# A gated MLP's gate and up projections with tokens as the stationary operand, turned back through 32x32 transposes and DRAM

## The chip, the cores and the metric

The kernel runs on one core of one Trainium2 chip. The metric is the device time of one execution in microseconds (us). The engines are TensorE (PE: matmuls; PEld: its weight loads), VectorE (DVE), ScalarE (ACT), GpSimd (POOL) and SyncE (SP). DMAs are issued by SP and by ACT, and one set of 16 DMA engines carries them all.

## The reference

A trunk of two layers works on 256 tokens of width 2048, in float32: a mixer (layer 0: short convolution and a state-space scan; layer 1: windowed attention), cross-attention into 256 memory tokens, and a gated MLP of width 5632. The change is in the MLP:

```python
def causal_dwconv(u, w):
    L = u.shape[1]
    up = jnp.pad(u, ((0, 0), (CONV_WIDTH - 1, 0), (0, 0)))
    y = up[:, 0:L] * w[0]
    for k in range(1, CONV_WIDTH):
        y = y + up[:, k:k + L] * w[k]
    return y

def conv_gated_mlp(h, w_gate, w_up, conv_w, conv_b, w_down):
    g = causal_dwconv(h @ w_gate, conv_w) + conv_b
    return (jax.nn.silu(g) * (h @ w_up)) @ w_down
```

`h` here is the residual after an RMS norm; the MLP's result is added to the residual. The convolution runs along the tokens, three wide, with weights and a bias of its own for each of the 5632 channels.

## The kernel before, in words

Activations lie with channels on the 128 partitions and the 256 tokens along a partition. A float32 product is made of three float32r products: operands are split into hi and lo, and hi x hi, hi x lo and lo x hi are summed. An activation tile `op` holds hi in its first 256 columns and lo in its last 256 (`split_gain`, L67 and L68; `split`, L74 and L75). Weights come from HBM in pieces of 1 MB or less: `wload` (L78) issues the load on SP into one of three `raw` buffers, ACT makes `hi` (L90) and DVE makes `lo` (L91), four buffers of 1024 columns each. So a load can start when the DVE subtract has read a raw buffer, and a cast when the matmuls have read a hi buffer.

`gemm` (L119) takes one output tile of 128 channels after another. For each it runs, over K contraction tiles, a matmul with the weight's hi stationary and all 512 columns of `op` moving (`mm_hi`, L105), and then one with the weight's lo stationary and the 256 hi columns moving (`mm_lo`, L110). The two halves of the PSUM bank are added by ACT and DVE (`add_halves`, L160 and L161). PSUM has four such banks (`pp`).

The norm's factor per token is not known when the projections begin. `stat_col` (L178) sums the squares on PE (L186) and takes the inverse root; `stat_bc` (L207) spreads it over partitions as `rbc`. In the MLP (`mlp`, L909) the first two tiles are held one contraction tile short (`late`, `pre`), with `stat_col` behind them. GpSimd multiplies gate by `rbc` (L918); ACT and DVE do the convolution (L920 to L922) and ACT the silu (L923); GpSimd multiplies by `rbc` again (L924) and then up by gate (L930); the product is split (L74, L75) into `ops`.

The 44 tiles of the width go in four slabs of 11. The down projection of a slab (16 output tiles, 11 contraction tiles each) adds to the residual `h` (`resid_part`, L961 and L962); the last slab of a layer also begins the next norm (`resid_evac`: L288, L289, `stat_add` with L174 on ACT and L172 on GpSimd, and `split_gain`). One pair of the next slab is computed ahead of each down projection.

The memory's V projection (`mem_kv`, L311 to L329) is of another form: tokens are stationary and 512 weight columns move (L319, L320, L324), into two banks.

A scheduler orders the instructions of every engine before the run; an engine takes its queue in that order, and an instruction that waits holds those behind it. This is so for DMA issues too.

## Time and profile before

| | |
|---|---|
| median of three runs | 2825.39 us (2824.67 to 2825.44) |
| the profiled execution | 2825.51 us |
| its span, first to last instruction | 2823.7 us |
| granted TensorE clock | 0.997 |
| DMA moved | 536.74 MB, mean 190 GB/s |
| 1 MB weight load, issue to landing | 4.8 us |

A profile row names the line, the engine, the operation, the tiles written and read, the shapes, the count, the busy time and the mean length of one in ns; behind the second bar stands the engine's idle time ahead of these instructions and what ended most of it. A timeline row begins with the start and the length in us. Lengths of matmuls are modelled and overlap; the distance of starts is what one costs.

### The profile page before, as it was taken

The page shows a single profiled execution, that of the slowest core. Times are in us where ns is not written, and L with a number is a line of the kernel's source. Part 1 is how long each engine was busy: PE and PEld are TensorE (multiplying, and loading weights), DVE is VectorE, ACT ScalarE, POOL GpSimd, SP SyncE. Part 2 cuts the span into 40 slices and gives each one's busy share as a digit, 9 for nine tenths or more (in the row PEclk, how much of TensorE's full clock was granted, in tenths as well). Part 3 has the DMA queues.
Part 4 walks back from the last instruction along what each step waited for, and adds up shares of the span by engine and source line. Part 5 has one row for each costly group of instructions (what it writes and reads, how often), then busy time and mean ns, then how long its engine had stood idle before and what let it go on. Part 6 is the DMA issues. An engine that isn't in the chain of part 4 may idle for free.

```text
span 2823.7 us, 43952 instructions
## 1 busy us (share of the span) xinstructions
PE 2797.2 (99%) x17159; PEld 2487.4 (88%) x17159; DVE 1956.9 (69%) x3171; ACT 1566.1 (55%) x2520; POOL 358.2 (13%) x397
## 2 busy tenths in 40 slices
PE   9999999999999999999999999999999999999998
PEld 8988979998988888888888888889888888888887
DVE  8878778767766666666666778776666666666666
ACT  7676766655555545545445566555555455454454
POOL 1000000001001211202112310000122012021122
PEclk9999999999999999999999999999999999999999
DMA  8564655555545555455555554454455554654544
GB/s 304 203 220 166 214 213 191 206 181 203 190 174 185 193 169 212 176 199 192 170 204 179 193 183 152 163 209 179 166 193 185 174 208 166 208 193 167 206 171 143
DMA packets 89794, 536.74 MB, mean 190 GB/s; under 512 B 10640, under 2 KB 17136, under 8 KB 38640
## 3 DMA queue, kind: packets, MB, share of 16 engines
q1 hardware_dynamic: 86656, 524.66, 52.7%
q10 hardware_dynamic: 2928, 9.26, 0.8%
q8 instruction: 134, 2.20, 0.3%
q14 instruction: 76, 0.62, 0.1%
HBM read 523.35 MB, written 10.53 MB: 189 GB/s over the span
## 4 chain that ended last, share of the span: by engine, by line
PE 93%; DVE 3%; ACT 2%; DMA 1%; issue 0%; SPq 0%; POOL 0%; DVEq 0%; ACTq 0%; POOLq 0%
PE ps L105 49%; PE ps L110 28%; PE ps L102 3%; PE ps L103 2%; PE ps L319 2%; PE ps L320 2%; PE ps L324 2%; DVE lo L91 1%; PE m L881 1%; ACT stmp L489 1%; PE m L787 1%; DVE stmp L493 1%; DMA kv<-kst 1%; ACT hi L90 0%; DVE S L494 0%
## 5 line engine op out<-in xcount | busy, mean ns | idle before, releaser
L91 DVE TENSOR_TENSOR lo<-raw,hi 128x1024 fp32r<-128x1024 f32 (+2 forms) x1033 | 1202.0, 1185 | 408.4 <-ACT hi L90 151.6
L105 PE MATMUL ps<-op,hi 128*128 128x512 f32 x6101 | 1471.5, 392 | 1.9 <-DVE op L75 1.1
L90 ACT CAST hi<-raw 128x1024 fp32r<-128x1024 f32 (+2 forms) x1033 | 1002.7, 983 | 818.1 <-PE ps L105 694.1
L105 PEld LDWEIGHTS ps<-op,hi 128*128 128x128 f32 x6101 | 1117.9, 188 | 220.9 <-issue 3.2
L110 PEld LDWEIGHTS ps<-op,lo 128*128 128x128 f32 x7008 | 900.4, 191 | 33.5 <-DVE lo L91 1.6
L110 PE MATMUL ps<-op,lo 128*128 128x256 f32 x7008 | 920.5, 283 | 1.4 <-DVE lo L91 1.4
L172 POOL TENSOR_TENSOR acc<-acc,t 128x256 f32<-128x256 f32 x98 | 89.4, 912 | 1194.7 <-ACT t L174 1190.7
L102 PE MATMUL ps<-op,hi 128*128 128x256 f32 x907 | 223.6, 286 | 6.7 <-ACT hi L90 6.6
L103 PE MATMUL ps<-op,hi 128*128 128x256 f32 x907 | 221.4, 284 | 0.0
L102 PEld LDWEIGHTS ps<-op,hi 128*128 128x128 f32 x907 | 174.8, 193 | 10.1 <-ACT hi L90 8.5
L103 PEld LDWEIGHTS ps<-op,hi 128*128 128x128 f32 x907 | 174.9, 193 | 0.1
L160 ACT COPY t<-ps 128x256 f32<-128x256 f32 x234 | 86.4, 372 | 151.6 <-PE ps L110 148.8
L918 POOL TENSOR_TENSOR t<-t,rbc 128x256 f32<-128x256 f32 x88 | 68.6, 780 | 749.2 <-DVE t L161 721.4
L921 DVE SCALAR_TENSOR_TENSOR t<-t,ff_conv 128x255 f32<-128x255 f32 x88 | 42.9, 488 | 141.9 <-ACT t L920 141.9
L924 POOL TENSOR_TENSOR t<-t,rbc 128x256 f32<-128x256 f32 x88 | 109.2, 1240 | 216.5 <-ACT t L923 216.5
L68 DVE SCALAR_TENSOR_TENSOR op<-h,gains,op 128x256 fp32r<-128x256 f32 x96 | 73.0, 768 | 88.4 <-ACT op L67 88.2
L489 ACT ACTIVATE stmp<-S,s_pw 128x256 f32<-128x256 f32 (+3 forms) x256 | 118.4, 530 | 28.3 <-DVE S L496 24.9
L75 DVE TENSOR_TENSOR op<-t,op 128x256 fp32r<-128x256 f32 x104 | 43.9, 424 | 116.6 <-ACT op L74 116.5
L319 PE MATMUL ps<-hi,op 128*128 128x512 f32 x256 | 101.0, 394 | 0.3 <-ACT hi L90 0.3
L320 PE MATMUL ps<-hi,op 128*128 128x512 f32 x256 | 99.9, 390 | 0.0
L161 DVE TENSOR_TENSOR t<-ps,t 128x256 f32<-128x256 f32 x226 | 93.9, 416 | 0.0
L930 POOL TENSOR_TENSOR t<-t 128x256 f32<-128x256 f32 x88 | 66.8, 759 | 135.1 <-DVE t L161 134.8
(213 smaller groups left out, 1705.7 us busy)
## 6 DMA issues: line engine op xcount, KB each, us to landing
raw<-in_ff_gate SPq DMA_DIRECT2D x88, 1024.0 KB, 4.8
raw<-in_ff_up SPq DMA_DIRECT2D x88, 1024.0 KB, 4.8
raw<-in_ff_down SPq DMA_DIRECT2D x128, 704.0 KB, 4.1
raw<-in_xa_k SPq DMA_DIRECT2D x32, 1024.0 KB, 4.9
raw<-in_xa_v SPq DMA_DIRECT2D x32, 1024.0 KB, 4.9
raw<-in_xa_q SPq DMA_DIRECT2D x32, 1024.0 KB, 4.8
raw<-in_xa_o SPq DMA_DIRECT2D x32, 1024.0 KB, 4.8
raw<-in_ev_w_in SPq DMA_DIRECT2D x28, 1024.0 KB, 4.9
```

The lines of the kernel that those rows point to most:

```text
L90: nc.scalar.copy(hi, s)
L91: nc.vector.tensor_tensor(lo, s, hi.bitcast(F32), op=ALU.subtract)
L102: nc.tensor.matmul(ps[:, :T], lhsT=hi, rhs=o[:, :T], start=k == 0, stop=False)
L103: nc.tensor.matmul(ps[:, :T], lhsT=hi, rhs=o[:, T:], start=False, stop=False)
L105: nc.tensor.matmul(ps, lhsT=hi, rhs=o, start=k == 0, stop=False)
L110: self.nc.tensor.matmul(ps[:, :T], lhsT=w[k][1], rhs=ops[k][:, :T], start=False, stop=k == K - 1)
L161: self.nc.vector.tensor_tensor(out, ps[:, :T], t, op=ALU.add)
L172: nc.gpsimd.tensor_tensor(self.acc, self.acc, self.sq, op=ALU.add)
L319: nc.tensor.matmul(ps[b], lhsT=o[:, b * P:(b + 1) * P], rhs=w[j][0], start=k == 0, stop=False)
L320: nc.tensor.matmul(ps[b], lhsT=o[:, T + b * P:T + (b + 1) * P], rhs=w[j][0], start=False, stop=False)
L489: nc.scalar.activation(tmp[:, x, :, p - p0, :], at(0, both, p), AF.Copy, scale=pw[:, x, k, 8 * b + p:8 * b + p + 1])
L924: nc.gpsimd.tensor_tensor(y, y, self.rbc, op=ALU.mult)
```

## The change

Tiles 0 to 39 of gate and up (of 44) take the form of the V projection. `tok_gemm` loads 512 weight columns for four contraction tiles at a time (the same 1 MB as before) and runs, for the even and the odd tokens (b), two matmuls of 512 columns with the weight's hi moving (x hi and x lo stationary) and one with its lo moving. Even and odd tokens are picked by every second column of `op` (`tokens`). Both products go to the same bank, so `add_halves` falls away for them, and the norm's factor is applied per partition by ACT as it evacuates (`tok_turn`). The result has tokens on partitions: DVE transposes it in 32x32 blocks, four DMAs on ACT's queue write it to DRAM (`zd`, runs of 256 bytes), and one DMA on SP's queue reads it back (`zf`, runs of 1 KB) with channels on partitions. The convolution, silu, product and split follow on `zf`, without the products with `rbc`. Tiles 40 to 43 stay in the old form, so `rbc` is still made, with its tokens in order again.

The slabs become 12, 12, 12 and 8 tiles: chunks (of four tiles) 0 to 3, down of 0 to 11; chunks 4 to 6, down; chunks 7 to 9, down; four old pairs, down of the last eight. `stat_col` comes behind the first quarter of the first chunk.

```diff
--- before.py
+++ after.py
@@ -26,7 +26,7 @@
 KT = 16
 DFF = 5632
 NFF = 44
-SLAB = 11
+NTOK = 40
 EPS = 1e-5
 MAGIC = 12582912.0
 XSCALE = 512 ** -0.5
@@ -49,6 +49,7 @@
         self.pp = pool("pp", 4, space=PSUM)
         self.pm = pool("pm", 4, space=PSUM)
         self.dp = pool("dram", 1, space=DRAM)
+        self.dz = pool("dramz", 4, space=DRAM)
     def t1(self, shape=(P, T), dt=F32):
@@ -155,6 +156,47 @@
             n, w, ps = start(i, K)
             finish(n, ps)
+    @staticmethod
+    def tokens(x, b):
+        return x.rearrange("p (m b) -> p b m", b=2)[:, b]
+    def tok_gemm(self, src, xs, after=None):
+        nc = self.nc
+        ps = [self.pp.tile([P, 512], F32, name="ps", tag="ps") for _ in range(2)]
+        for q in range(4):
+            w = self.wload(src(q), 4, 512)
+            for j in range(4):
+                k = 4 * q + j
+                for b in range(2):
+                    for i in range(2):
+                        nc.tensor.matmul(ps[b], lhsT=self.tokens(xs[k][:, i * T:(i + 1) * T], b), rhs=w[j][0], start=k == 0 and i == 0, stop=False)
+            for j in range(4):
+                k = 4 * q + j
+                for b in range(2):
+                    nc.tensor.matmul(ps[b], lhsT=self.tokens(xs[k][:, :T], b), rhs=w[j][1], start=False, stop=k == KT - 1)
+            if after is not None:
+                after(q)
+        return ps
+    def tok_turn(self, pool, ps, rcol, tag):
+        nc = self.nc
+        tt = pool.tile([P, 16, 32, 2], F32, name="tt", tag="tt")
+        for b in range(2):
+            z = pool.tile([P, 512], F32, name="zt", tag="zt")
+            nc.scalar.activation(z, ps[b], AF.Copy, scale=rcol[:, b:b + 1])
+            nc.vector.transpose(tt[:, :, :, b], z.rearrange("p (j i) -> p j i", i=32))
+        zd = self.dz.tile([512, T], F32, name="zd", tag="zd")
+        for q in range(4):
+            nc.scalar.dma_start(zd.rearrange("(j i) (q e) -> q i j e", i=32, q=4)[q], tt[32 * q:32 * q + 32].rearrange("p j i b -> p j (i b)"))
+        zf = pool.tile([P, 4, T], F32, name="zf", tag=tag)
+        nc.sync.dma_start(zf, zd.rearrange("(n p) t -> p n t", p=P))
+        return zf
     def add_halves(self, out, ps):
         t = self.t1()
         self.nc.scalar.copy(t, ps[:, T:])
@@ -175,7 +217,7 @@
         self.sq = t
         self.accn += 1
-    def stat_col(self, tag="h", apart=False):
+    def stat_col(self, tag="h", apart=False, turned=False):
         nc = self.nc
         ps = self.bank()
@@ -183,7 +225,7 @@
             nc.gpsimd.tensor_tensor(self.acc, self.acc, self.sq, op=ALU.add)
         for b in range(2):
             c = slice(b * P, (b + 1) * P)
-            nc.tensor.matmul(ps[:, b:b + 1], lhsT=self.acc[:, c], rhs=self.ones[:, :1], start=True, stop=not apart)
+            nc.tensor.matmul(ps[:, b:b + 1], lhsT=self.tokens(self.acc, b) if turned else self.acc[:, c], rhs=self.ones[:, :1], start=True, stop=not apart)
             if apart:
                 nc.tensor.matmul(ps[:, b:b + 1], lhsT=self.sq[:, c], rhs=self.ones[:, :1], start=False, stop=True)
         return self.rsqrt_col(ps[:, :2], tag)
@@ -204,7 +246,7 @@
         self.rcol = y
         return y
-    def stat_bc(self, tag="h", copy=True):
+    def stat_bc(self, tag="h", turned=False):
         nc = self.nc
         diag = self.t1()
@@ -213,7 +255,10 @@
         pb = self.bank()
         nc.tensor.matmul(pb[:, :T], lhsT=self.ones, rhs=diag, start=True, stop=True)
         rbc = self.smp.tile([P, T], F32, name="rbc", tag="rbc_" + tag, bufs=1)
-        nc.scalar.copy(rbc, pb[:, :T])
+        if turned:
+            nc.scalar.copy(rbc.rearrange("p (m b) -> p b m", b=2), pb[:, :T].rearrange("p (b m) -> p b m", b=2))
+        else:
+            nc.scalar.copy(rbc, pb[:, :T])
         self.rbc = rbc
         return rbc, pb
@@ -930,31 +975,62 @@
             nc.gpsimd.tensor_tensor(z, z, st["y"], op=ALU.mult)
             st["ops"].append(self.split(z))
-        def pairs(ns, pre=0):
-            items = [x for n in ns for x in ((0, n), (1, n))]
-            self.gemm(lambda i: I["ff_up" if i[0] else "ff_gate"][l, i[1]], items, xs, KT,
-                      lambda i, ps: (evac_up if i[0] else evac_gate)(i[1], ps), late=1 if pre else 0, pre=pre, mid=self.stat_col if pre else None, mid2=self.stat_bc if pre else None)
-        nxt = None
-        ops = []
-        st["ops"] = ops
-        pairs(range(0, SLAB), pre=2)
-        for s in range(4):
-            cur = ops
-            if s < 3:
-                ops = []
-                st["ops"] = ops
-                pairs(range(SLAB * (s + 1), SLAB * (s + 1) + 1))
+        def pair(n):
+            w = n - NTOK
+            self.gemm(lambda i: I["ff_up" if i else "ff_gate"][l, w], (0, 1), xs, KT, lambda i, ps: (evac_up if i else evac_gate)(n, ps))
+        def chunk(c):
+            first = c == 0
+            def after(q):
+                if first and q == 0:
+                    st["rcol"] = self.stat_col(turned=True)
+                if first and q == 2:
+                    self.stat_bc(turned=True)
+            g = self.tok_turn(pool, self.tok_gemm(lambda q: I["ff_gate_t"][l, c, q], xs, after), st["rcol"], "zg")
+            ys = []
+            for i in range(4):
+                n = 4 * c + i
+                z = g[:, i, :]
+                y = pool.tile([P, T], F32, name="y", tag="y")
+                nc.scalar.activation(y, z, AF.Identity, scale=cw[:, l, n, 2:3], bias=cb[:, l, n:n + 1])
+                v.scalar_tensor_tensor(y[:, 1:], z[:, :T - 1], cw[:, l, n, 1:2], y[:, 1:], op0=ALU.mult, op1=ALU.add)
+                v.scalar_tensor_tensor(y[:, 2:], z[:, :T - 2], cw[:, l, n, 0:1], y[:, 2:], op0=ALU.mult, op1=ALU.add)
+                nc.scalar.activation(y, y, AF.Silu)
+                ys.append(y)
+            u = self.tok_turn(pool, self.tok_gemm(lambda q: I["ff_up_t"][l, c, q], xs), st["rcol"], "zu")
+            for i in range(4):
+                nc.gpsimd.tensor_tensor(u[:, i, :], u[:, i, :], ys[i], op=ALU.mult)
+                st["ops"].append(self.split(u[:, i, :]))
+        def down(s, k0, k1, cur):
             if s == 3:
                 evac, nxt = self.resid_evac(gnext)
             else:
-                ev, _ = (lambda n, ps: self.resid_part(n, ps)), None
-                evac = ev
-            self.gemm(lambda n: I["ff_down"][l, s, n], range(16), cur, SLAB, evac, one=lambda n: s == 3 and gnext is None and n == KT - 1)
-            if s < 3:
-                pairs(range(SLAB * (s + 1) + 1, SLAB * (s + 2)))
-        return nxt
+                evac, nxt = self.resid_part, None
+            self.gemm(lambda n: I["ff_down"][l, n][:, k0:k1, :], range(16), cur, k1 - k0, evac, one=lambda n: s == 3 and gnext is None and n == KT - 1)
+            return nxt
+        with tc.tile_pool(name=f"ff{l}", bufs=2) as pool0:
+            class pool:
+                @staticmethod
+                def tile(shape, dt, name, tag):
+                    return pool0.tile(shape, dt, name=name, tag=tag, bufs=6 if tag == "y" else 2)
+            ops = st["ops"] = []
+            for c in range(4):
+                chunk(c)
+            down(0, 0, 12, ops[:12])
+            for c in range(4, 7):
+                chunk(c)
+            down(1, 12, 24, ops[12:24])
+            for c in range(7, 10):
+                chunk(c)
+            down(2, 24, 36, ops[24:36])
+            for n in range(NTOK, NFF):
+                pair(n)
+            return down(3, 36, 44, ops[36:])
     def resid_part(self, n, ps):
         h = self.h[n]
@@ -1065,9 +1141,11 @@
     A["xa_k"] = np.stack([_tiles(x[:, :D], P) for x in g["xa_w_kv"]])
     A["xa_v"] = np.stack([x[:, D:].reshape(4, 4, P, 4, 512).transpose(3, 0, 2, 1, 4) for x in g["xa_w_kv"]])
     A["xa_o"] = np.stack([_tiles(x, P) for x in g["xa_w_o"]])
-    A["ff_gate"] = np.stack([_tiles(x, P) for x in g["ff_w_gate"]])
-    A["ff_up"] = np.stack([_tiles(x, P) for x in g["ff_w_up"]])
-    A["ff_down"] = np.stack([x.reshape(4, SLAB, P, KT, P).transpose(0, 3, 2, 1, 4) for x in g["ff_w_down"]])
+    tok = lambda w: np.stack([x[:, :NTOK * P].reshape(4, 4, P, NTOK // 4, 512).transpose(3, 0, 2, 1, 4) for x in w])
+    A["ff_gate_t"], A["ff_up_t"] = tok(g["ff_w_gate"]), tok(g["ff_w_up"])
+    A["ff_gate"] = np.stack([_tiles(x[:, NTOK * P:], P) for x in g["ff_w_gate"]])
+    A["ff_up"] = np.stack([_tiles(x[:, NTOK * P:], P) for x in g["ff_w_up"]])
+    A["ff_down"] = np.stack([_tiles(x, P) for x in g["ff_w_down"]])
     A["ff_conv"] = _cols(g["ff_conv_w"]).transpose(0, 1, 3, 2)
     A["ff_b"] = _cols(g["ff_conv_b"])
     A["flip"] = np.eye(P, dtype=np.float32)[::-1]
```

On SP, in the MLP of layer 0 around a down projection, before (`raw` buffers are loaded, nothing else):

```order
L82 DMA raw<-in_ff_up 128x2048
L82 DMA raw<-in_ff_down 128x1408 x16
L82 DMA raw<-in_ff_gate 128x2048
L82 DMA raw<-in_ff_up 128x2048
L82 DMA raw<-in_ff_gate 128x2048
```

And now, from the first gate load of chunk 3 on (line numbers are those of the changed kernel; L197 is the read of `zf`):

```order
L83 DMA raw<-in_ff_gate_t 128x2048
L197 DMA zf<-zd 128x4x256
L83 DMA raw<-in_ff_gate_t 128x2048 x3
L83 DMA raw<-in_ff_up_t 128x2048
L197 DMA zf<-zd 128x4x256
L83 DMA raw<-in_ff_up_t 128x2048 x3
L83 DMA raw<-in_ff_down 128x1536
L197 DMA zf<-zd 128x4x256
L83 DMA raw<-in_ff_down 128x1536 x5
L197 DMA zf<-zd 128x4x256
L83 DMA raw<-in_ff_down 128x1536 x10
```

Each `zf` stands one load behind the projection that follows the one it belongs to: the read of a gate result is behind the up projection's four loads and the first of the next gate's, and ahead of the other three.

On ACT, in steady gate and up pairs, before (casts between evacuations and the steps of the convolution):

```order
L160 COPY t<-ps 128x256
L90 CAST hi<-raw 128x1024
L74 CAST op<-t 128x256
L90 CAST hi<-raw 128x1024
L160 COPY t<-ps 128x256
L90 CAST hi<-raw 128x1024
L920 ACTIVATE t<-t,ff_b,ff_conv 128x256
L90 CAST hi<-raw 128x1024
L923 ACTIVATE t<-t 128x256
```

And now, from the evacuation of a gate projection to that of its up projection (L191 evacuates, L195 issues the writes to `zd`, L997 waits for `zf`, L1000 is the silu):

```order
L191 ACTIVATE zt<-ps,rcol 128x512 x2
L91 CAST hi<-raw 128x1024
L195 DMA zd<-tt 32x16x64 x4
L91 CAST hi<-raw 128x1024 x5
L997 ACTIVATE y<-zf,ff_b,ff_conv 128x256 x4
L1000 ACTIVATE y<-y 128x256
L91 CAST hi<-raw 128x1024
L1000 ACTIVATE y<-y 128x256 x3
L91 CAST hi<-raw 128x1024
L191 ACTIVATE zt<-ps,rcol 128x512 x2
```

The evacuations come once per 512 columns, and the steps of the convolution for four tiles stand together, five casts behind the writes.

## The prediction

> **What bounds the kernel now.** I read the page's busy times and chain first, then TensorE's timeline in three stages, then what fills the buffers. The page's first part, and the head of its chain:
>
> ```profile
> PE 2797.2 (99%) x17159; PEld 2487.4 (88%) x17159; DVE 1956.9 (69%) x3171; ACT 1566.1 (55%) x2520; POOL 358.2 (13%) x397
> ...
> PE 93%; DVE 3%; ACT 2%; DMA 1%; issue 0%; SPq 0%; POOL 0%; DVEq 0%; ACTq 0%; POOLq 0%
> ```
>
> TensorE (PE) is on the path nearly everywhere; VectorE (DVE) and ScalarE (ACT) have slack on average. So the change pays where it alters the pace of matmuls, and costs where it makes PE wait. Busy shares don't tell the pace, since modelled matmul ends overlap; starts do. TensorE's timeline (start, length, line, form) in the MLP of layer 0:
>
> ```profile
> 1144.77 3.82 PE L105 MATMUL ps<-op,hi 128*128 128x512 f32 x16
> 1148.42 2.08 PE L110 MATMUL ps<-op,lo 128*128 128x256 f32 x16
> 1150.34 3.82 PE L105 MATMUL ps<-op,hi 128*128 128x512 f32 x16
> 1153.99 2.08 PE L110 MATMUL ps<-op,lo 128*128 128x256 f32 x16
> 1155.90 3.82 PE L105 MATMUL ps<-op,hi 128*128 128x512 f32 x16
> ```
>
> One 128-column tile takes 1155.90 - 1150.34 = 5.56 us; over the two tiles it is 11.13 / 2 = 5.565. Sixteen matmuls of 512 columns take 3.65, sixteen of 256 take 1.91: 119.4 ns each, more than half of a 512. The change replaces them by the form that the memory's V projection has (L319 to L324: tokens stationary, 512 weight columns moving). Its timeline, where nothing disturbs it:
>
> ```profile
> 431.47 0.39 PE L319 MATMUL ps<-hi,op 128*128 128x512 f32 x1
> ...
> 435.10 1.98 PE L324 MATMUL ps<-lo,op 128*128 128x512 f32 x8
> 436.91 0.39 PE L319 MATMUL ps<-hi,op 128*128 128x512 f32 x1
> ...
> 440.54 1.98 PE L324 MATMUL ps<-lo,op 128*128 128x512 f32 x8
> 442.35 0.28 PE L102 MATMUL ps<-op,hi 128*128 128x256 f32 x1
> ```
>
> Four contraction tiles times 512 columns, 24 matmuls, take 5.44 us twice over: 226.7 ns each. That is the same arithmetic as one 128-column tile over all 16 contraction tiles.
>
> **The change part by part.** *Matmul forms.* Gate and up of 40 of 44 tiles, in two layers, are 160 such units. Each goes from 5.565 to 5.44: 160 x 0.125 = 20.0 us saved. The saving is the per-matmul overhead: 24 starts where there were 32. An estimate for a worse end: next to busy neighbours a V quarter's first sixteen ran
>
> ```profile
> 425.86 0.50 PE L319 MATMUL ps<-hi,op 128*128 128x512 f32 x1
> ...
> 429.66 1.98 PE L324 MATMUL ps<-lo,op 128*128 128x512 f32 x8
> ```
>
> in 3.80 us instead of 3.63 (with about 0.1 of a cold start); at that pace, 231 ns, the unit would take 5.55 and nearly nothing would be saved. I take 5.44, since the MLP has no scan beside it.
>
> *Stationary operand.* Its columns are now every second word of `op`. No row shows a strided weight load. Bounds: with 256 columns moving a contiguous load is hidden within 119.4 ns, so at most that; at half the rate it takes up to 238.8, which is 12.1 over the 226.7 pace, 24 x 160 x 12.1 ns = 46 us. A gain is excluded, since the contiguous load is hidden already. I take zero. The Trainium skill (Advanced Engine Details and Errata, SBUF Cachelines) says that two hits in a 16-byte line suffice for full rate, and this stride gives two; no run here shows it.
>
> *Engines beside.* Out go L160, L161, L918 and L924; in come two evacuations (L191) and two 32x32 transposes (L192) per 512 columns. Nearest rows:
>
> ```profile
> L328 ACT ACTIVATE kst<-ps,rcol 128x512 f32<-128x512 f32 x16 | 10.1, 682 | 1.6 <-PE ps L324 1.6
> L494 DVE TENSOR_TENSOR S<-S,stmp 128x512 f32<-128x512 f32 x28 | 24.6, 881 | 12.9 <-ACT stmp L489 12.9
> L870 DVE TENSOR_TENSOR pT<-m,pT 128x512 fp32r<-128x512 f32 x8 | 5.5, 683 | 5.2 <-ACT pT L869 5.2
> L91 DVE TENSOR_TENSOR lo<-raw,hi 128x1024 fp32r<-128x1024 f32 x903 | 1131.1, 1275 | 406.8 <-ACT hi L90 149.9 <-PE ps L110 146.7 <-issue 71.5
> L90 ACT CAST hi<-raw 128x1024 fp32r<-128x1024 f32 x903 | 945.0, 1051 | 816.6 <-PE ps L105 694.1 <-PE ps L103 43.2 <-issue 39.2
> L921 DVE SCALAR_TENSOR_TENSOR t<-t,ff_conv 128x255 f32<-128x255 f32 x88 | 42.9, 488 | 141.9 <-ACT t L920 141.9
> ```
>
> DVE per 512 gate columns: 8 x 1.275 + 2 x (0.68 to 0.88) + 8 x 0.49 = 15.5 to 15.9 of 21.76 us. ACT has less. Neither becomes the bound on average.
>
> *DMA traffic.* Per 512 columns the turn writes 2048 runs of 256 bytes and reads 512 of 1 KB. The DMA answers for an MLP window (1078.13 to 1144.93) and an attention window with bias loads in 1 KB rows (1669.86 to 1755.19):
>
> ```profile
> DMA packets 1854, 13.62 MB, mean 204 GB/s; under 512 B 194, under 2 KB 194, under 8 KB 194
> q1 hardware_dynamic: 1851, 13.57, 56.7%
> ```
>
> ```profile
> DMA packets 4212, 13.44 MB, mean 158 GB/s; under 512 B 336, under 2 KB 2896, under 8 KB 2896
> q1 hardware_dynamic: 4202, 13.32, 44.8%
> bias<-fd SPq DMA_DIRECT2D x10, 256.0 KB, 3.2
> ```
>
> First: 16 x 66.80 x 0.567 = 606 us over some 1657 packets of 8 KB: 366 ns each. Second: 612 us, less 1280 x 0.366, leaves 143 for 2560 packets of 1 KB: 56 ns each. A 256-byte write lies between its share of bytes (366/32 = 11) and, if size doesn't matter, 56. Engine time per 512 columns: weights 512 x 366/16 = 11.7 us, reads 1.8, writes 1.5 to 7.2: 15.0 to 20.7 of 21.76. It fits, tightly at the top; I take 30 ns, about the middle, 17.3 in all.
>
> *The waits in the queues.* The order shows `zf` on SP behind the four weight loads of the next projection and one of the projection after it, ahead of that one's other three; on ACT the four writes stand one cast behind the evacuations, and the conv's four activations five casts later. Call the end of a projection's matmuls 0. ACT evacuates by 1.4, DVE transposes by about 3, ACT issues four writes at 0.33 each by 4.2.
>
> ```profile
> kv<-kst ACTq DMA_DIRECT2D x16, 512.0 KB, 4.1
> raw<-in_ff_gate SPq DMA_DIRECT2D x88, 1024.0 KB, 4.8
> ```
>
> ```profile
> 1163.10 0.33 SPq L82 DMA_DIRECT2D raw<-in_ff_up  x1
> ```
>
> A write of the same bytes lands 4.1 after issue; with up to 7.2 of packet time and 2.9 of a weight load between, 14.2. So writes land at 8 to 18.5, and `zf` 3.5 to 5 later, at 12 to 23.5. Who waits: on SP the next loads. A load is due when its raw buffer is free, for the quarter after the queued one at about 7.4 (one quarter, 5.44, plus cast and subtract), and PE needs it at five quarters, 27.2. Issued after `zf` at 18.5 and landing 5 later, then cast in 1.05, it is still in time; the limit is writes landing at 20. On ACT the five casts are paced by PE and end near 15.5, so the activations hardly wait; the next cast is due at 18.1 but needed only by 26. I cost the turn at nothing, under a cover of up to 12 us; where that is gone each us costs 40.
>
> *Down and slabs.* Contractions go from 11 x 4 to 12, 12, 12, 8. The matmul count stays. Before, a tile of 11:
>
> ```profile
> 1020.47 2.68 PE L105 MATMUL ps<-op,hi 128*128 128x512 f32 x11
> 1022.99 1.48 PE L110 MATMUL ps<-op,lo 128*128 128x256 f32 x11
> 1024.30 2.68 PE L105 MATMUL ps<-op,hi 128*128 128x512 f32 x11
> ```
>
> 3.65 for 16 and 2.52 for 11 give 0.226 each and 0.03 a switch, so a tile of 8 takes 2.80. In the last slab of layer 0, DVE per tile had
>
> ```profile
> 1584.47 1.23 DVE L91 TENSOR_TENSOR lo<-raw,hi 128x1024 fp32r<-128x1024 f32 x1 [0.60 <-ACT t L174]
> ...
> 1585.62 0.96 DVE L68 SCALAR_TENSOR_TENSOR op<-h,gains,op 128x256 fp32r<-128x256 f32 x1
> 1586.50 0.41 DVE L288 TENSOR_TENSOR h<-h,ps 128x256 f32<-128x256 f32 x1
> ...
> 1586.83 0.55 DVE L91 TENSOR_TENSOR lo<-raw,hi 128x384 fp32r<-128x384 f32 x1
> ...
> 1587.30 0.41 DVE L289 TENSOR_TENSOR h<-h,ps 128x256 f32<-128x256 f32 x1
> ```
>
> Without the 0.55 that is 3.01 for 2.80 of PE: DVE becomes the bound for 16 tiles, 3.4 us lost (0 to 8: buffers may cover it, or the 0.60 gap stays). Layer 1 has no L68 there, and loses nothing. The slab's start waits on the last pair's product, twice:
>
> ```profile
> 1560.15 0.50 PE L105 MATMUL ps<-op,hi 128*128 128x512 f32 x1 [0.56 <-DVE op L75]
> ```
>
> Seven matmuls now stand ahead of it instead of ten: 2 x 3 x 0.226 = 1.4 us lost.
>
> *Start of a layer.* The norm's matmul L186 moves from behind two held tiles to behind the first quarter, 5.4 us after the residual's last matmul. It needs L288, L289, L174 and two sums on GpSimd:
>
> ```profile
> L174 ACT ACTIVATE t<-h 128x256 f32<-128x256 f32 x105 | 42.2, 410 | 12.9 <-DVE h L289 12.0
> L172 POOL TENSOR_TENSOR acc<-acc,t 128x256 f32<-128x256 f32 x98 | 89.4, 912 | 1194.7 <-ACT t L174 1190.7 <-ACT hi L90 3.4
> ```
>
> 0.41 x 3 + 2 x 0.91 = 3.1, which fits. Zero, at worst 2 us each.
>
> Sum on the profiled execution (2825.51, its span of 2823.7 and 1.8 around it): -20.0 + 3.4 + 1.4 = -15.2, so 2810.3; it stands 0.1 above the median of 2825.39, so 2810.
>
> **The rivals.** *DMA engines become the bound (slower).* If a 256-byte write costs over (21.76 - 11.7 - 1.8) x 16 / 2048 = 65 ns, PE starves in every projection; each 10 ns beyond costs 1.28 us a turn, 51 in all. At twice the 56, 112 ns: 27.8 against 21.76, 40 x 6.0 = 242 us, 3052. For it: 56 is close to 65, and all known packets are larger. Against: the 56 holds a whole KB. The Trainium skill (DMA: Bandwidth & Descriptors, Specifications) has such a rule: below 512 bytes an engine reads, modifies and writes. It gives no price, and no row here has such a write. Chance 0.08.
>
> *Slow strided weight loads (slower).* Decides from a load interval over 226.7 ns; at 238.8, 2810 + 46 = 2856. Every matmul of L175 and L179 would be spaced alike. Chance 0.07.
>
> *The turn's latency (slower).* Writes landing at over 20 us with the engines not full: at 21, 40 us, 2850. Chance 0.05.
>
> *The saving is eaten.* The pace stays near 5.5, or small waits come in each chunk: half or more of the 20 us go, 2816 to 2830. Chance 0.10, half of it within 0.2% of before.
>
> *The forecast*, 2804 to 2817: chance 0.70.
>
> **How the numbers follow.** A measurement of this kernel can tell about 0.2%, 5.6 us. Faster: 0.70 + 0.05 = 0.75. Within: 0.05. Slower: 0.08 + 0.07 + 0.05 = 0.20. The range goes from the forecast's best (all 20 us and none of the losses, 2805, and 2 for a start of the layer that gains) to the end of the eaten saving, 2830: 0.80.
>
> **What would show it.** Right: L175 and L179 spaced at 226 to 228 ns, no PE idle time ahead of them, writes landing by 15 us after a projection's end, a DMA share near 0.8 in gate and up, and DVE waits in layer 0's last slab. Wrong: spacing over 230; idle PE released by casts or subtracts once per projection; SP waiting for `zd` beyond 20 us.

## The result and the profile after

The changed kernel takes 2832.13 us (median of 10 runs) where the kernel before takes 2825.49 (10 runs, 2824.67 to 2826.28): ratio 1.0023, 95% interval 1.0013 to 1.0032. It was forecast 15 us faster and is 6.6 us slower. One run of the ten, at 9471.91 us, lies outside all others and is left out of the ratio; without it the median is 2831.88. The profiled execution took 2831.88 us, its span is 2829.7 (2823.7 before), its granted clock 0.997 as before.

The page of the changed kernel, first part, head of the chain, and the two groups of the new matmuls (L175 moves the weight's hi, L179 its lo; the last column is PE's idle time ahead of them):

```profile
PE 2801.8 (99%) x15876; PEld 2441.2 (86%) x15876; DVE 1903.2 (67%) x3059; ACT 1551.3 (55%) x2408; POOL 209.4 (7%) x237
...
PE 93%; DVE 4%; ACT 2%; DMA 1%; issue 1%; SPq 0%; POOL 0%; DVEq 0%; ACTq 0%; POOLq 0%
...
L175 PE MATMUL ps<-hi,op 128*128 128x512 f32 x2560 | 623.5, 394 | 0.0
...
L179 PE MATMUL ps<-lo,op 128*128 128x512 f32 x1280 | 324.4, 394 | 0.0
```

PE issues 1283 matmuls fewer and never waits ahead of the new ones: 0.0 us over 3840 of them. No new wait has taken the gain. So the pace is to be read, from TensorE's timeline in the first chunk's up projection:

```profile
906.11 3.89 PE L175 MATMUL ps<-hi,op 128*128 128x512 f32 x16
...
911.71 3.89 PE L175 MATMUL ps<-hi,op 128*128 128x512 f32 x16
```

A quarter of a projection, the unit of the prediction, takes 911.71 - 906.11 = 5.60 us, 24 matmuls at 233.3 ns. Forecast was 5.44, at 226.7; the old form took 5.565. That is nearly the whole result: 160 x (5.60 - 5.565) = +5.6 us. The weight loads' records differ too: those of L175, whose stationary columns are every second word of `op`, have a median of 193 ns, contiguous ones under the same 512 columns (L106) 188. It is a lead and no proof, since contiguous loads under 256 moving columns show 192.

The turn: ACT's timeline at the end of a projection, whose matmuls have ended where the evacuation (L191) starts, and SP's row of the read back:

```profile
995.67 1.27 ACT L191 ACTIVATE zt<-ps,rcol 128x512 f32<-128x512 f32 x2 [0.58 <-PE ps L179]
...
1011.80 1.58 ACT L997 ACTIVATE y<-zf,ff_b,ff_conv 128x256 f32<-128x256 f32 x3
```

```profile
1005.54 0.38 SPq L197 DMA_DIRECT2D zf<-zd  x1
```

The read back is issued 1005.54 - 995.67 = 9.9 us after the projection's end, and the convolution (L997) starts behind a cast, without a wait for `zf`.

### The profile page after: what moved, and what is told of

Read it like the earlier page. It is cut to its first block, busy times and chain, and to the rows that moved or that the text cites. A ratio compares the mean times of both kernels' runs of the same rounds, so it can differ in the third digit from the quotient of the medians.

```text
span 2829.7 us, 41446 instructions
## 1 busy us (share of the span) xinstructions
PE 2801.8 (99%) x15876; PEld 2441.2 (86%) x15876; DVE 1903.2 (67%) x3059; ACT 1551.3 (55%) x2408; POOL 209.4 (7%) x237
## 4 chain that ended last, share of the span: by engine, by line
PE 93%; DVE 4%; ACT 2%; DMA 1%; issue 1%; SPq 0%; POOL 0%; DVEq 0%; ACTq 0%; POOLq 0%
PE ps L106 29%; PE ps L175 21%; PE ps L111 17%; PE ps L179 11%; PE ps L103 3%; PE ps L104 3%; PE ps L364 2%; PE ps L365 2%; PE ps L369 2%; DVE lo L92 1%; PE m L926 1%; ACT stmp L534 1%; PE m L832 1%; DVE stmp L538 1%; DMA raw<-in_ev_u 0%
## 5 line engine op out<-in xcount | busy, mean ns | idle before, releaser
L92 DVE TENSOR_TENSOR lo<-raw,hi 128x1024 fp32r<-128x1024 f32 (+1 forms) x1001 | 1161.0, 1178 | 654.3 <-issue 295.9
L91 ACT CAST hi<-raw 128x1024 fp32r<-128x1024 f32 (+1 forms) x1001 | 996.2, 1007 | 949.7 <-PE ps L106 418.3
L106 PE MATMUL ps<-op,hi 128*128 128x512 f32 x3544 | 860.3, 392 | 2.9 <-DVE op L76 1.9
L106 PEld LDWEIGHTS ps<-op,hi 128*128 128x128 f32 x3544 | 648.3, 188 | 131.4 <-issue 3.2
L175 PE MATMUL ps<-hi,op 128*128 128x512 f32 x2560 | 623.5, 394 | 0.0
L111 PEld LDWEIGHTS ps<-op,lo 128*128 128x128 f32 x4448 | 571.9, 191 | 21.1 <-DVE lo L92 1.7
L111 PE MATMUL ps<-op,lo 128*128 128x256 f32 x4448 | 587.8, 283 | 1.5 <-DVE lo L92 1.5
L175 PEld LDWEIGHTS ps<-hi,op 128*128 128x128 f32 x2560 | 493.6, 193 | 102.4
L179 PE MATMUL ps<-lo,op 128*128 128x512 f32 x1280 | 324.4, 394 | 0.0
L179 PEld LDWEIGHTS ps<-lo,op 128*128 128x128 f32 x1280 | 247.0, 193 | 51.6
L103 PEld LDWEIGHTS ps<-op,hi 128*128 128x128 f32 x904 | 175.0, 194 | 10.2 <-ACT hi L91 8.6
L104 PEld LDWEIGHTS ps<-op,hi 128*128 128x128 f32 x904 | 175.0, 194 | 0.1
L364 PE MATMUL ps<-hi,op 128*128 128x512 f32 x256 | 101.1, 395 | 0.4 <-ACT hi L91 0.3
L365 PE MATMUL ps<-hi,op 128*128 128x512 f32 x256 | 99.9, 390 | 0.0
L369 PE MATMUL ps<-lo,op 128*128 128x512 f32 x256 | 63.2, 389 | 0.0
```

What stands on the lines that cost most here:

```text
L91: nc.scalar.copy(hi, s)
L92: nc.vector.tensor_tensor(lo, s, hi.bitcast(F32), op=ALU.subtract)
L103: nc.tensor.matmul(ps[:, :T], lhsT=hi, rhs=o[:, :T], start=k == 0, stop=False)
L104: nc.tensor.matmul(ps[:, :T], lhsT=hi, rhs=o[:, T:], start=False, stop=False)
L106: nc.tensor.matmul(ps, lhsT=hi, rhs=o, start=k == 0, stop=False)
L111: self.nc.tensor.matmul(ps[:, :T], lhsT=w[k][1], rhs=ops[k][:, :T], start=False, stop=k == K - 1)
```

## The experiments

Theory A: the strided stationary operand costs 6.6 ns a matmul. Theory B, its rival: the turn's traffic and the engines' reads and writes beside TensorE slow the matmuls. The first four kernels part these.

**Column step by chunk.** The stationary columns lie 1, 2, 3 and 4 words apart in chunks 0, 1, 2 and 3, and so on round.

```diff
+    STEPS = (1, 2, 3, 4)
+    def stat(self, x, i, b, c):
+        s = self.STEPS[c % 4]
+        if s <= 2:
+            y = x[:, i * T:(i + 1) * T]
+            return self.tokens(y, b) if s == 2 else y[:, b * P:(b + 1) * P]
+        return x[:, b:b + s * (P - 1) + 1:s]
```

> The changed kernel, with another set of stationary columns in each chunk: chunk number modulo 4 gives a column step of 1, 2, 3 or 4 words (step 1: two contiguous blocks; steps 3 and 4 pick 128 columns out of all 512), so the gate and up results hold other tokens than the reference's; matmuls, loads, turns and their order stay. Theory A (the strided weight load itself costs): quarters of 24 matmuls at 5.44 us in the chunks of step 1, at 5.60 in those of step 2, and more than 5.60 at steps 3 and 4 if the cost grows with the step. Theory B (the turn's DMA traffic or its writes into the same memory slow the matmuls): 5.60 in all chunks, whatever the step, since the turn is in all of them. Total by A: 12 of 40 projections in layer pairs come at 5.44, so some 48 x 0.16 = 8 us below the changed kernel if steps 3 and 4 cost no more than 2.

2826.79 us in one run. TensorE's timeline, two starts of a quarter in each of chunks 0, 1 and 2:

```profile
904.56 3.79 PE L184 MATMUL ps<-hi,op 128*128 128x512 f32 x16
...
910.00 3.79 PE L184 MATMUL ps<-hi,op 128*128 128x512 f32 x16
...
931.93 3.89 PE L184 MATMUL ps<-hi,op 128*128 128x512 f32 x16
...
937.53 3.89 PE L184 MATMUL ps<-hi,op 128*128 128x512 f32 x16
...
982.42 3.93 PE L184 MATMUL ps<-hi,op 128*128 128x512 f32 x16
...
988.08 3.94 PE L184 MATMUL ps<-hi,op 128*128 128x512 f32 x16
```

Quarters take 5.44, 5.60 and 5.66 us at steps 1, 2 and 3, and 5.63 at step 4 (1033.27 to 1038.90): 0, 6.7, 9 and 8 ns per matmul. The chunks with step 1 have the same turn beside them and run at 5.44, so theory B is false. The cost does not grow with the distance past step 3. The whole run is 5.3 us below the changed kernel where 8 was expected, since steps 3 and 4 cost more than step 2.

**Step 2 without a turn.** The kernel before, with every second column as stationary operand in the memory's V projection alone.

```diff
-matmul(ps[b], lhsT=o[:, b * P:(b + 1) * P], rhs=w[j][0], start=k == 0, stop=False)
+matmul(ps[b], lhsT=o[:, b:T:2], rhs=w[j][0], start=k == 0, stop=False)
```

(and likewise for the two others). 

> The kernel before, with every second column as stationary in the memory's V projection alone (L319, L320, L324), where the step was 1; V's rows then hold the memory tokens in another order than the probabilities do, so the cross-attention's values are not the reference's. No turn through DRAM anywhere. Theory A: undisturbed quarters of that projection go from 5.44 to 5.60 us; 32 quarters make at most 5 us in all, 2830. Theory B: they stay at 5.44, and the time at 2825.

2828.07 us in one run. The V projection's timeline:

```profile
366.86 2.03 PE L324 MATMUL ps<-lo,op 128*128 128x512 f32 x8
...
372.46 2.03 PE L324 MATMUL ps<-lo,op 128*128 128x512 f32 x8
```

5.60 us a quarter, in a kernel with no turn, where the contiguous form took 5.44. Theory A holds by itself. The whole run is 2.2 us slower than the kernel before, where 5 was the most expected.

**Narrower lo matmuls.** The changed kernel with only 256 columns moving in the lo matmuls; step 1 in even chunks, step 2 in odd ones. It asks whether the cost is the load's own length or something added to every matmul.

```diff
-matmul(ps[b], lhsT=self.tokens(xs[k][:, :T], b), rhs=w[j][1], start=False, stop=k == KT - 1)
+matmul(ps[b][:, :T], lhsT=self.stat(xs[k], 0, b, c), rhs=w[j][1][:, :T], start=False, stop=k == KT - 1)
```

> The changed kernel with only 256 of 512 columns moving in the matmuls of the weights' lo part (half of that small correction is left out), and a contiguous stationary operand in even chunks (tokens in two blocks there, so other tokens than the reference's), a step of 2 in odd ones. It asks what the step costs. Theory A1 (a fixed 6.6 ns a matmul): the narrow matmuls are spaced at 119.5 ns in even chunks and at 126 in odd ones. Theory A2 (the strided load takes 233 ns and is the bound in place of the 226.7 of the moving columns): 119.5 in even chunks, 233 in odd ones. Theory B (traffic of the turn): the same in both, some 126.

2701.72 us in one run. Its timeline, an even chunk and then an odd one (L183 is lo):

```profile
910.25 3.82 PE L179 MATMUL ps<-hi,op 128*128 128x512 f32 x16
913.90 1.12 PE L183 MATMUL ps<-lo,op 128*128 128x256 f32 x8
914.85 3.82 PE L179 MATMUL ps<-hi,op 128*128 128x512 f32 x16
...
924.13 3.93 PE L179 MATMUL ps<-hi,op 128*128 128x512 f32 x16
927.90 1.12 PE L183 MATMUL ps<-lo,op 128*128 128x256 f32 x8
928.86 3.93 PE L179 MATMUL ps<-hi,op 128*128 128x512 f32 x16
```

Eight lo matmuls take 0.95 and 0.96 us, the same within the records' hundredth; sixteen hi take 3.65 and 3.77. None of the three expectations was met: with 256 columns moving the step costs nothing, with 512 it costs 7 ns. The strided load is not simply longer than a matmul's interval, or it would have shown first at the shorter one.

**Contiguous stationary columns.** The changed kernel, with even and odd tokens put side by side when the operand is split, and the order turned back where the four old pairs are added up. All else as in the change.

```diff
-    def split_gain(self, src, gcol):
+    def split_gain(self, src, gcol, turned=False):
+        hi, lo, hf = o[:, :T], o[:, T:], o[:, :T].bitcast(F32)
+        if turned:
+            src = src.rearrange("p (m b) -> p b m", b=2)
+            hi, lo, hf = (x.rearrange("p (b m) -> p b m", b=2) for x in (hi, lo, hf))
...
-matmul(ps[b], lhsT=self.tokens(xs[k][:, i * T:(i + 1) * T], b), rhs=w[j][0], ...
+matmul(ps[b], lhsT=xs[k][:, i * T + b * P:i * T + (b + 1) * P], rhs=w[j][0], ...
```

> The changed kernel with the split of the activations that writes even tokens first and odd ones behind them, so that the stationary operand is contiguous; the four old pairs put their sums back in order as DVE adds the halves. All else, the turn through DRAM too, as in the changed kernel. Theory A: quarters at 5.44, 160 x 0.16 = 25.6 us below the changed kernel, 2806.5. Theory B: quarters at 5.60, 2832. A risk in both: ACT and DVE take longer over the reordered split, beside the last cross-attention projection, which would show as PE waiting at the start of the MLP.

2807.82 us (5 runs, 2806.71 to 2808.05) beside 2825.91 for the kernel before: ratio 0.9936, interval 0.9922 to 0.9949. Timeline, a quarter, and the first matmuls of layer 0's MLP and of what follows it:

```profile
883.60 3.82 PE L179 MATMUL ps<-hi,op 128*128 128x512 f32 x16
...
906.34 3.79 PE L179 MATMUL ps<-hi,op 128*128 128x512 f32 x16
...
911.78 3.79 PE L179 MATMUL ps<-hi,op 128*128 128x512 f32 x16
...
1610.83 3.59 PE L110 MATMUL ps<-op,hi 128*128 128x512 f32 x15
```

The quarter is at 5.44, and the changed kernel's 24.3 us loss against this one is the step's price: 160 x 0.16 = 25.6. This version is faster than both kernels, 0.6% below the one before.

**The turn left out.** The same version, but the transposed blocks are used as they lie, with no pass through DRAM.

```diff
-        zd = self.dz.tile([512, T], F32, name="zd", tag="zd")
-        for q in range(4):
-            nc.scalar.dma_start(...)
-        zf = pool.tile([P, 4, T], F32, name="zf", tag=tag)
-        nc.sync.dma_start(zf, zd.rearrange("(n p) t -> p n t", p=P))
-        return zf
+        return tt.rearrange("p (n j) i b -> p n (j i b)", n=4)
```

> The version with contiguous stationary columns (2807.8 us), but the pass through DRAM is left out: the transposed blocks are taken as they lie in the tile, in a wrong order, so no writes, no read back, and the convolution follows the transposes directly. It asks what the turn costs in all. Theory 1, the turn lies wholly beside the matmuls: within 1.5 us of 2807.8, quarters at 5.44. Theory 2, it costs something that the profile's waits don't show (traffic beside the weight loads, or the queues): 2803 or less, some 0.12 us or more per turn, 40 turns.

2806.11 us (5 runs, 2805.08 to 2807.84), ratio 0.9932 (0.9918 to 0.9945): the intervals overlap widely. Its timeline at the same two places:

```profile
881.44 3.82 PE L179 MATMUL ps<-hi,op 128*128 128x512 f32 x16
...
1608.67 3.36 PE L110 MATMUL ps<-op,hi 128*128 128x512 f32 x14
```

1608.67 - 881.44 = 727.23 us without the pass, 1610.83 - 883.60 = 727.23 with it. The turn costs nothing in layer 0; the 2 us between the profiled runs lie ahead of the MLP. In layer 1, too, the first and the last of the new matmuls start 569.71 us apart in both.

**Writes three times, on ACT's queue.** The version with contiguous columns; each write of the turn is followed by two more to places that nothing reads.

```diff
+        for r in range(2):
+            ze = self.dz.tile([512, T], F32, name="ze", tag=f"ze{r}")
+            for q in range(4):
+                nc.scalar.dma_start(ze.rearrange(...)[q], tt[32 * q:32 * q + 32]...)
```

> The version with contiguous stationary columns (2807.8 us), with every write of the turn made three times (twice to places that nothing reads). 4096 more packets of 256 bytes per turn, at 17.8 ns over 16 engines, are 4.6 us more engine time per 21.76 us, so a DMA share near 0.88 in gate and up where it was 0.67, and 4.1 us more of issuing on ACT. Theory 1, there is cover for that: within 3 us of 2807.8. Theory 2, the turn as it is already stands near the limit, through the engines or through ACT's queue: PE idles once per chunk behind casts, 1 us or more per turn, 2848 or more.

3128.11 us (4 runs), ratio 1.107 (1.1055 to 1.1085). PE's waits ahead of the new matmuls (us, times, longest), then ACT's timeline around a turn, then TensorE's after the first wait:

```profile
PE ps L179 <- ACT hi L95: 190.1, 34, 8.6
```

```profile
971.86 2.19 ACTq L199 DMA_DIRECT2D zd<-tt  x4
974.08 7.37 ACTq L203 DMA_DIRECT2D ze<-tt  x8
983.56 2.08 ACT L1009 ACTIVATE y<-zf,ff_b,ff_conv 128x256 f32<-128x256 f32 x4 [11.59 <-DMA ze<-tt]
```

```profile
927.38 3.78 PE L179 MATMUL ps<-hi,op 128*128 128x512 f32 x8 [8.60 <-ACT hi L95]
930.96 2.14 PE L183 MATMUL ps<-lo,op 128*128 128x512 f32 x8
```

By the time alone, the second theory. But the rows show what the expectation had not reckoned with: the scheduler put the convolution (L1009) directly behind the writes, where five casts had stood between. ACT issues for 9.6 us and then waits for `zf`, casting nothing, and PE starves. (The row names a write of `ze`, which landed close by; `zf` was issued at 978.88 and took some 4.7 to land.) These waits and 38.5 us of like ones at the line of the other projections (L110) make 229 of the 320 us. Much of the rest is a slower TensorE behind each wait: the eight matmuls from 927.38 take 3.58 us instead of 1.81, at a granted clock of 0.50 there, and 0.958 over the run where its base has 0.997. So the run mixes two causes, the traffic and ACT's queue, and the next one parts them.

**The extra writes on GpSimd's queue.** The same, with the two extra sets issued by GpSimd.

```diff
-                nc.scalar.dma_start(ze.rearrange(...)[q], tt[32 * q:32 * q + 32]...)
+                nc.gpsimd.dma_start(ze.rearrange(...)[q], tt[32 * q:32 * q + 32]...)
```

> The version with contiguous stationary columns (2807.8 us), with the turn's writes made three times again (twice to places that nothing reads), but the extra ones issued by GpSimd, so that ACT's queue holds casts behind the writes as before. It parts the two things that tripled writes on ACT's queue mixed (3128 us, at a DMA share of only 0.67 and with no cast between the writes and the convolution). Theory 1, the 320 us came from ACT's queue: here PE stays fed, within 5 us of 2807.8, at a DMA share near 0.88 in gate and up. Theory 2, they came from the write packets: PE again waits some 6 us or more per turn behind casts, 3050 or more.

2807.26 us (4 runs), ratio 0.9937 (0.9922 to 0.9952), the same as without extra writes. Engines' busy times in a stretch of gate and up (PE, PEld, DVE, ACT, POOL; the last columns are granted clock, DMA share, GB/s), of this run and then of the version with contiguous columns:

```profile
906.11:1061.00 154.89, 154.89 (x686) 128.27 (x685) 91.41 (x116) 83.92 (x118) 45.92 (x68) 1.00 0.81 274
```

```profile
906.11:1061.00 154.89, 154.89 (x685) 128.26 (x684) 98.03 (x118) 86.49 (x118) 12.17 (x12) 1.00 0.69 231
```

At three times the bytes written and a DMA share of 0.81 instead of 0.69, PE is busy without a gap. So the 320 us came from ACT's queue, and the DMA engines were no bound. Whether the longer issuing or the changed order did it, the two runs don't part. Nor does this run triple the small packets: in the DMA answer for the window 927 to 1014 GpSimd's queue shows 1536 packets for 4.20 MB, 2.7 KB each on average. The run before did triple them, on ACT's queue, whose row of the same answer is (packets, MB, share of 16 engines):

```profile
q10 hardware_dynamic: 18792, 4.67, 23.2%
```

There they took 16 x 87 x 0.232 / 18792 = 17.2 ns each, and weight loads of gate and up landed 4.9 and 5.0 us after issue, where the base has 5.8. So the small packets did not hold up the loads.

This run tests the turn's cover as well. The reads back go out 10.5 to 20.0 us after their projection's end (median 13.7; in the base 8.4 to 11.3, median 10.5), and no projection takes longer than in the base.

**One pass more.** The version with contiguous columns; GpSimd's queue copies `zd` to another place in DRAM, and the read back is from there, so it comes later.

```diff
+        ze = self.dz.tile([512, T], F32, name="ze", tag="ze")
+        nc.gpsimd.dma_start(ze, zd)
-        nc.sync.dma_start(zf, zd.rearrange("(n p) t -> p n t", p=P))
+        nc.sync.dma_start(zf, ze.rearrange("(n p) t -> p n t", p=P))
```

> The version with contiguous stationary columns (2807.8 us), with one more pass in DRAM: after the writes GpSimd's queue copies the turned block to another place, and the read back takes it from there. It lengthens the turn by a transfer of 512 KB, by 4 to 6 us from the rows of the read, and adds 1 MB of traffic. SP's order keeps the read behind the next projection's four loads and, now, two of the one after. Theory 1, the cover reckoned in the prediction, that the read may start up to 20 us after a projection's end where it now starts at about 10: within 3 us of 2807.8. Theory 2, the cover is nearly used up: 1 us or more per turn, 2848 or more.

2835.38 us (5 runs, 2831.27 to 2839.64), ratio 1.0035 (1.0021 to 1.0049): 28 us over its base, between the two expectations. PE's waits ahead of casts in down and gate or up, then ACT's timeline at the start of the first down projection and TensorE's first wait there:

```profile
PE ps L110 <- ACT hi L95: 17.9, 16, 2.2
...
PE ps L179 <- ACT hi L95: 2.8, 3, 1.6
```

```profile
1062.23 2.08 ACT L1007 ACTIVATE y<-zf,ff_b,ff_conv 128x256 f32<-128x256 f32 x4 [7.81 <-DMA zf<-ze]
```

```profile
1065.61 3.01 PE L110 MATMUL ps<-op,hi 128*128 128x512 f32 x12 [0.99 <-ACT hi L95]
```

Inside gate and up, PE still hardly waits (L179, 2.8 us); ahead of the down projections it does (L110, 17.9). There ACT stands at the convolution (L1007) until `zf` lands; the next cast of down weights is behind it, from 1064.53 to 1065.56, and PE starts when it ends. A down tile of 12 takes 4.18 us, where a quarter of gate or up takes 5.44. The reads go out later than the added pass alone makes them. In a turn amid gate and up (projection's end at 992.83, read back at 1013.66) it is 20.8 us instead of 9.9, because ACT had waited for the turn before (5.05 us, ahead of L79) and evacuated only at 999.47. Over all turns it is 14.0 to 21.7 us, median 18.4. Gate and up lose 4.3 us by it, nearly all of it in three projections that follow reads at 19.9 us and later; the two down projections of each layer that stand between chunks lose 15.4 together (70.6 to 70.8 us each instead of 66.85); most of the rest is lost behind the last chunk of each layer.

**From what width the step costs.** Two runs of the changed kernel with the lo matmuls at other widths, two chunks each, step 1 in even and 2 in odd chunks.

```diff
+    WIDE = (128, 256, 320, 384, 448)
...
+        m = self.WIDE[c // 2]
...
+matmul(ps[b][:, :m], lhsT=self.stat(xs[k], 0, b, c), rhs=w[j][1][:, :m], start=False, ...
```

> The changed kernel, but the matmuls with the weight's lo move only the first 128, 256, 320, 384 or 448 of its 512 columns (chunks 0 and 1, 2 and 3, 4 and 5, 6 and 7, 8 and 9), and their and the hi matmuls' stationary columns are contiguous in even chunks and every second one in odd chunks; the rest of lo is left out, and the tokens of even chunks are others than the reference's. It asks from what moving width the step costs. Known: nothing at 256 columns (119 ns each with and without it), 6.7 ns at 512. Theory 1, a limit just above 256: odd chunks lose 6.7 ns per lo matmul at 320, 384 and 448 alike (eight lo matmuls take 0.05 us more). Theory 2, a cost that grows with the columns past 256: 1.7, 3.3 and 5.0 ns, so 0.01, 0.03 and 0.04 us per eight. Theory 3, a strided load only costs at the full 512: nothing at all three. By all three the sixteen hi matmuls keep 3.63 us in even and about 3.75 in odd chunks.

In the second, the widths are 480, 496, 504, 508 and 510.

> As the run with lo matmuls of 128 to 448 columns, now with 480, 496, 504, 508 and 510 columns (two chunks each, contiguous stationary columns in even chunks, every second column in odd ones; the rest of lo is left out, and the tokens of even chunks are others than the reference's). There the step cost nothing at 256 to 448 columns and 6.7 ns per hi matmul of 512. Theory 1, the cost belongs to the full 512: no difference between even and odd chunks in the lo matmuls at all five widths. Theory 2, it sets in between 448 and 512: eight lo matmuls of an odd chunk take 0.01 to 0.05 us more from some width on.

They took 2734.64 and 2814.45 us, one run each. The first run at 128 columns, an even and an odd chunk:

```profile
909.60 1.00 PE L186 MATMUL ps<-lo,op 128*128 128x128 f32 x8
910.44 3.90 PE L182 MATMUL ps<-hi,op 128*128 128x512 f32 x16
...
928.05 1.05 PE L186 MATMUL ps<-lo,op 128*128 128x128 f32 x8
928.94 3.95 PE L182 MATMUL ps<-hi,op 128*128 128x512 f32 x16
```

Eight lo matmuls take 0.84 and 0.89 us, 105 and 111 ns each. A matmul of 256 columns takes 119 and half as many columns hardly less, so here the load seems to set the pace (an inference, no row shows it), and the strided one to be 6 ns longer. At 320, 384 and 448 columns the two steps are within 0.02 us per eight. The second run at 510 columns, even and odd:

```profile
1398.61 1.98 PE L186 MATMUL ps<-lo,op 128*128 128x510 f32 x8
1400.42 3.79 PE L182 MATMUL ps<-hi,op 128*128 128x512 f32 x16
...
1443.03 2.03 PE L186 MATMUL ps<-lo,op 128*128 128x510 f32 x8
1444.89 3.89 PE L182 MATMUL ps<-hi,op 128*128 128x512 f32 x16
```

Here 1.81 and 1.86 us, 0.05 more with the step; at 480 it was 0.03, at 496 0.04, at 504 and 508 nothing. So none of the expected laws holds: the cost is there at 128, gone from 256 to 448, there at 480 and 496, gone at 504 and 508, and there at 510 and 512. Why some widths hide it and others don't stays open; what is shown is the price at 512 columns, the only width that the change uses.

## Why the prediction was wrong, point by point

**The step that failed** is the one on the stationary operand, "I take zero." It costs 6.7 ns on each of 24 x 160 matmuls, 25.6 us, and lay between the bounds given for it (zero to 46). I took zero because nothing in the profile showed such a load, and let the end without a measurement stand for the middle. The sum with that term put right, and with the two smaller ones below, is 2825.51 - 20.0 + 25.6 + 0.8 = 2831.9, and the profiled execution took 2831.88. That it fits so closely is partly luck: 0.7 us of the difference lies ahead of layer 0's MLP (first matmul at 882.83 instead of 882.14), for which the sum has no term. The rule cited there, of the Trainium skill (Advanced Engine Details and Errata, SBUF Cachelines), was read as saying that two hits in a 16-byte line suffice for full rate; the page says "Need at least two hits on a cacheline to absorb SRAM access latency". It is no licence for zero here: step 2 gives two hits, and it costs 6.7 ns at 512 moving columns. Of the rival "slow strided weight loads" the price came, at 233.3 ns, and its sign, L175 and L179 all spaced alike. Its mechanism is not shown: it takes a load that itself lasts over 226.7 ns, but with 256 columns moving the strided load fits into 119 ns. The same goes for the bounds in the sum, which were worked out from such a load. How the step comes to cost 6.7 ns stays open.

**Fewer matmul starts** was right and right in size: with contiguous columns the unit takes the forecast 5.44 us. There the median fell by 18.1 us; in layer 0 the MLP takes 727.23 instead of 1619.08 - 882.14 = 736.94, 9.7 less, of 80 x 0.125 = 10.0 and a slab's start. The timeline of before for these two ends:

```profile
882.14 3.59 PE L105 MATMUL ps<-op,hi 128*128 128x512 f32 x15
...
1619.08 3.59 PE L105 MATMUL ps<-op,hi 128*128 128x512 f32 x15
```

**DVE in layer 0's last slab**, a loss of 3.4 us, did not come. The changed kernel's DVE there:

```profile
1593.63 0.96 DVE L69 SCALAR_TENSOR_TENSOR op<-h,gains,op 128x256 fp32r<-128x256 f32 x1
1594.51 0.41 DVE L334 TENSOR_TENSOR h<-h,ps 128x256 f32<-128x256 f32 x1
1594.94 0.42 DVE L333 TENSOR_TENSOR h<-h,ps 128x256 f32<-128x256 f32 x1
1595.28 1.22 DVE L92 TENSOR_TENSOR lo<-raw,hi 128x1024 fp32r<-128x1024 f32 x1
1596.42 0.96 DVE L69 SCALAR_TENSOR_TENSOR op<-h,gains,op 128x256 fp32r<-128x256 f32 x1
```

The four lengths add up to 3.01, as I reckoned, but from start to start they take 2.79: DVE's instructions overlap in the records as PE's do, so their cost is the distance of starts too. At PE's 2.80 a tile DVE is full and not late.

**The slabs' starts** cost less than the 1.4 us forecast. PE's waits for the last pair's product, after and before:

```profile
PE ps L106 <- DVE op L76: 1.9, 2, 0.9
```

```profile
PE ps L105 <- DVE op L75: 1.1, 2, 0.6
```

0.8 us more in two waits. The start of a layer cost nothing, as taken: no wait stands ahead of the new matmuls.

**The turn at nothing** was right, shown by the run without the pass. **Its cover** was right where it was worked out, for gate and up: I gave the writes up to 20 us from a projection's end to land. With the extra writes on GpSimd's queue reads went out up to 20.0 us after it and cost nothing; with one pass more they went out up to 21.7 and gate and up began to wait. I did not work the cover out for the down projections, and there it is shorter. ACT's casts of down weights stand behind the convolution and the split of the slab's last chunk, and a down tile is used up every 4.18 us. Reads of a slab's last chunk at up to 16.5 us cost nothing; at 18.3 and more they cost some 2 to 6 us a slab.

**The DMA engines** were never near their limit: their share in gate and up was 0.67, where the prediction named about 0.8. The price of a 256-byte write was taken as 30 ns, a threshold at 65. The writes' queue in the DMA answer for the window 927 to 1014 of the changed kernel (packets, MB, share of 16 engines):

```profile
q10 hardware_dynamic: 8448, 2.10, 10.8%
```

16 x 87 x 0.108 / 8448 = 17.8 ns each. The rule of the Trainium skill (DMA: Bandwidth & Descriptors, Specifications) that transfers under 512 bytes are read, modified and written did not make these writes dear: 17.8 ns is a third of the 56 of a 1 KB packet. (In the sum for those 56 the packets of 8 KB are 4202 - 2896 = 1306, not 1280, which gives 52 and changes nothing.)

## What to carry to other kernels

When a change alters how an operand lies in memory, that edit is an edit of its own: if no row shows it, forecast it inside its bounds and not at the end that costs nothing, since 6.7 ns on 3840 matmuls ate a gain of 20 us and more. Put the reordering where an engine writes the operand once (the split) and not where TensorE reads it again for every 512 weight columns. And reckon the cover of a wait for every kind of work that is queued behind it, on every engine, the fastest consumer first; durations of any engine are to be read from start to start.

## What the runs showed of the hardware

- A stationary operand with columns 2, 3 or 4 words apart makes a float32r matmul of 512 moving columns 6.7, 9 and 8 ns longer (226.7 ns contiguous). With 256 to 448, 504 and 508 moving columns (matmuls with the weight's lo) step 2 costs nothing; with 480, 496 and 510 it costs about 4, 5 and 6 ns.
- With 128 moving columns a matmul takes 105 ns, 111 with step 2; with 256 it takes 119.
- 256-byte writes to DRAM take 17.8 ns of a DMA engine each, 17.2 with three times as many. Tripling the bytes written by way of GpSimd's queue (DMA share 0.81) cost TensorE nothing; there the profile shows pieces of 2.7 KB on average.
- After an idle time of 8.60 us TensorE's granted clock was 0.50, and eight matmuls of 512 columns took 3.58 us instead of 1.81.
- Eight more DMA issues on ACT's queue took 7.37 us, 0.9 each, where the four ahead of them took 2.19 in all; and where a scheduler orders the queues, such an addition also moves what stands behind it.
